# Rotary scores over 128 rows with zero-padded keys, and three planner costs raised, in a two-layer hybrid decoder

## The chip, the core and the metric

The kernel runs on one core of one Trainium2 chip. The time is the device time of one execution in microseconds; of several runs the median counts. One execution was taken with the hardware profiler, and the rows below are from that one.

## The reference, cut

Two layers over 512 tokens of width 1024. Each layer is a half-step SwiGLU feed-forward (hidden width 2816), a mixer of three branches (gated DeltaNet, Conformer convolution, latent attention), and a second half-step feed-forward, with a layer norm behind each. The change is in the latent attention: its scores are the sum of a 128-wide product of each head and a 64-wide rotary product, whose key is shared by all four heads.

```python
def causal_block_attention(q_nope, q_rope, k_nope, k_rope, v):
    t = q_nope.shape[1]
    scale = (MLA_NOPE + MLA_ROPE) ** -0.5
    outs = []
    for i in range(t // ATTN_BLOCK):
        q0, q1 = i * ATTN_BLOCK, (i + 1) * ATTN_BLOCK
        s = (jnp.einsum('bqhd,bkhd->bhqk', q_nope[:, q0:q1], k_nope[:, :q1])
             + jnp.einsum('bqhr,bkr->bhqk', q_rope[:, q0:q1], k_rope[:, :q1])).astype(jnp.float32) * scale
        mask = jnp.arange(q1)[None, :] <= jnp.arange(q0, q1)[:, None]
        p = jax.nn.softmax(jnp.where(mask, s, -jnp.inf), axis=-1).astype(v.dtype)
        outs.append(jnp.einsum('bhqk,bkhv->bqhv', p, v[:, :q1]))
    return jnp.concatenate(outs, axis=1)
```

The DeltaNet branch squares and normalizes its keys and queries after a short convolution, and scales the keys by per-token factors; the planner costs that are raised are those of such scalings.

## The kernel before

Nothing is issued where it is written. Every engine instruction goes through a proxy into `Planner._record`, which notes an estimated cost in ns (`_cost`), what it reads and writes, and a priority: the running sum of TensorE costs at that place, plus a bias. `plan` then simulates the five queues with these costs, and at each point gives an engine the ready instruction of highest priority whose buffer is free. `issue` emits them all in the order of the simulated starts; this is why nearly every row of the profile has one line, L287. On the chip each engine runs its own list strictly in that order. So a changed cost or one changed instruction can move any instruction of the neighbourhood, and an instruction whose operands come later than planned holds up what stands behind it on its engine.

Most multiplications are three float32r products of a number split into a high and a low part (`mm3`, one TensorE instruction each). The scores, the products of the delta rule and P times V are in plain float32, for which TensorE runs two instructions per product. The tiles called `s` are slots of 128x512 float32 in SBUF, of which 76 rotate; `ps` are the eight PSUM banks; `xh` and `xl` are the two parts of the layer's input; `raw` are weights as loaded.

Each mixer begins with the key heads: projection, `short_conv` (a ScalarE scaling and three VectorE steps over 511, 510 and 509 columns, then a tanh and a product of 512 columns), transposes, and the squares. From the sums of squares VectorE makes the factors `rky`; ScalarE scales `ktok` by them in quarters (`scale_quarters`, 16 instructions a layer there), TensorE transposes the scaled quarters and makes `kk`; VectorE forms `U` and, in blocks of 32 partitions, `comp3`. Then the query heads go the same way: short convolution, and a group of four transposes per head.

In the attention part, head `h` and row block `i` of 128 tokens have `n = (i + 1) * 128` keys. `ps[:, 0:n]` gets two products: `qn[h]` with `kn[h]` over 128 rows of the array, and the rotary one over 64 rows. `qr[h // 2]` holds the rotary queries of an even head in partitions 0 to 63 and of the next odd head in 64 to 127; `krope` holds the same 64 key rows twice, in both halves. Then VectorE adds the mask, takes the maximum and scales it, ScalarE makes the exponentials and their sum, VectorE the reciprocal and the scaled P, TensorE transposes P, ScalarE copies it out, and TensorE multiplies with V (8 instructions a head, over 512, 384, 256 and 128 columns). Other work of VectorE is put between: splits of weights, and the 30 shifted steps for each of the four channel groups of the Conformer convolution.

Of the kernel before, what the change touches and what calls it, by code (L numbers as in the profile page):

```python
# [35 lines left out]
class Planner:  # L36
# [64 lines left out]
    def _cost(self, engine, name, outs, ins, k):  # L101
        o = outs[0]
        n = 1
        for d in o.shape[1:]:
            n *= d
        psum = any(x.space == bass.MemoryType.PSUM for x in ins)
        if engine == "PE":
            if name == "transpose":
                return 109.0
            if k["rhs"].dtype == F32R:  # L110
                return 13.4 + n / 2.4
            part = o.shape[0] < 128 or k["lhsT"].shape[0] < 128
            return max(8.0 + n / 0.6, 116.0) + (100.0 if part else 0.0)
        vectors = 0
        if engine in ("DVE", "POOL"):
            vectors = sum(x.free_size() == 1 for x in ins[1:])
            if n == 1:
                vectors = len(ins) - {"tensor_scalar": 1, "scalar_tensor_tensor": 2}.get(name, len(ins))
        if engine == "DVE":
            if name == "reciprocal":  # L120
                return 70 + 8.3 * n
            fast = name in ("tensor_scalar", "tensor_copy") and not psum
            if name in ("bn_stats", "bn_aggr", "reduce_max"):
                n = max(n, ins[0].free_size())
            return 70 + 57 * min(vectors, 1) + n * (0.52 if fast else 1.04)
        if engine == "ACT":
            c = (52 if psum else 94) + 0.83 * max(n, 64)
            if o.shape[0] < 128 and o.shape[0] % 32 == 0:
                c += 110
            c += 93 * sum(hasattr(k.get(x), "tensor") for x in ("scale", "bias", "accum_out"))  # L130
            return c
        if engine == "POOL":
            return 125 + n * {"tensor_tensor": 2.15, "tensor_scalar": 0.9}.get(name, 1.0)
        return max(500.0, n * o.shape[0] * 4 / 200.0)
# [209 lines left out]
def trunk(tc, a, out):  # L344
    pl = Planner(tc)

    with ExitStack() as ctx:
# [9 lines left out]
        def slot(dtype=F32, share=None):  # L357
            return pl.tile(s_p, [128, 512], dtype, "s", N_SLOTS, share)
# [16 lines left out]
        V, S, G, PE, Q = pl.V, pl.S, pl.G, pl.PE, pl.Q  # L375
# [380 lines left out]
        def mixer(l):  # L756
# [85 lines left out]
            for h in (2, 3):  # L842
                w = wcols(C_DK + h * 128)
                ps = bank()
# [14 lines left out]
            for h in range(H):  # L859
# [17 lines left out]
                for j in range(4):  # L877
                    u = 4 * h + j
                    c = slice(j * 128, (j + 1) * 128)
# [6 lines left out]
            for h in range(H):  # L886
                w = wcols(C_DQ + h * 128)
                ps = bank()
# [6 lines left out]
                for j in range(4):  # L895
                    c = slice(j * 128, (j + 1) * 128)
# [27 lines left out]
            for h in range(H):  # L924
                glu_taps(h)
                w = wcols(C_DV + h * 128)
                ps = bank()
# [45 lines left out]
            for h in range(H):  # L973
                y, x, n = spread(y3, h), spread(x3, h), slot()
# [9 lines left out]
            for tt in range(NT):  # L984
                o = slot()
                rs, vns, news = slot(), slot(), slot()
                c = slice(tt * 128, (tt + 1) * 128)
                for h in range(H):
                    u = 4 * h + tt
                    hc = slice(h * 128, (h + 1) * 128)  # L990
                    ps = bank()
                    q = quarters(ps)
                    rhs = vtok[h][:, c]
                    if tt:
# [3 lines left out]
                        rhs = r  # L998
# [50 lines left out]
            scale = small([128, 4], "scale", 1)  # L1049
# [3 lines left out]
            ps = bank()  # L1053
# [26 lines left out]
                S.copy(kr[64 * g:64 * g + 64], kr_sb[0:64])  # L1080
            krope = rope(kr, swapped(kr_sb, (0, 0)))


            og = []
            for h in range(H):
                w = wcols(C_DZ + h * 128)
                ps = bank()
# [7 lines left out]
            for h in range(H):  # L1095
                ps = bank()
# [6 lines left out]
            qn, qr, kn, vv = [], [], [], []  # L1103
# [45 lines left out]

            ao = []  # L1150
            for h in range(H):
                hr = slice(64 * (h % 2), 64 * (h % 2) + 64)
                pt = [slot() for _ in range(4)]
                for i in range(NT):
                    n = (i + 1) * 128
                    c = slice(i * 128, n)
                    ps = bank()
                    PE.matmul(ps[:, 0:n], lhsT=qn[h][:, c], rhs=kn[h][:, 0:n], start=True, stop=False)
                    PE.matmul(ps[:, 0:n], lhsT=qr[h // 2][hr, c], rhs=krope[hr, 0:n], start=False, stop=True)
                    V.tensor_tensor(ps[:, c], ps[:, c], C("amask"), op=ADD)  # L1160
                    mx = small([128, 1], "mx")
                    V.reduce_max(mx, ps[:, 0:n], axis=mybir.AxisListType.X)
                    V.tensor_scalar(mx, mx, scale[:, i:i + 1], -1.0, op0=MUL, op1=MUL)
                    p = slot()
                    rs = small([128, 1], "rs")
                    S.activation(p[:, 0:n], ps[:, 0:n], AF.Exp, scale=scale[:, i:i + 1], bias=mx, accum_out=rs)
                    V.reciprocal(rs, rs)
                    V.tensor_scalar(p[:, 0:n], p[:, 0:n], rs, None, op0=MUL)
                    tp = bank()
                    transposes(tp, quarters(p)[:i + 1])  # L1170
                    for j in range(i + 1):
                        S.copy(pt[j][:, c], quarters(tp)[j])
                ps = bank()
                for j in range(NT):
                    PE.matmul(ps[:, j * 128:], lhsT=vv[j][:, h * 128:(h + 1) * 128], rhs=pt[j][:, j * 128:],
                              start=j == 0, stop=j == NT - 1)
                ao.append(split(ps))
# [119 lines left out]
```

## Time and profile before

| what | value |
|---|---|
| median of 3 runs | 2466.42 us (2465.38 to 3408.69) |
| the profiled execution | 2464.4 us, span 2462.6 us |
| TensorE clock granted, mean | 0.998 |
| TensorE / VectorE / ScalarE / POOL busy | 99% / 83% / 51% / 0% |
| HBM | 108 GB/s over the span |

The span is the time from the first to the last instruction; the execution's own time lies 1.8 us above it. The third run, 3408.69 us, stands alone, and the median does not depend on it. In the profile PE is TensorE's multiplications and PEld its weight loads, DVE is VectorE, ACT ScalarE.

### The profile page before, as it was taken

The page shows a single profiled execution, that of the slowest core. Times are in us where ns is not written, and L with a number is a line of the kernel's source. Part 1 is how long each engine was busy: PE and PEld are TensorE (multiplying, and loading weights), DVE is VectorE, ACT ScalarE, POOL GpSimd, SP SyncE. Part 2 cuts the span into 40 slices and gives each one's busy share as a digit, 9 for nine tenths or more (in the row PEclk, how much of TensorE's full clock was granted, in tenths as well). Part 3 has the DMA queues.
Part 4 walks back from the last instruction along what each step waited for, and adds up shares of the span by engine and source line. Part 5 has one row for each costly group of instructions (what it writes and reads, how often), then busy time and mean ns, then how long its engine had stood idle before and what let it go on. Part 6 is the DMA issues. An engine that isn't in the chain of part 4 may idle for free.

```text
span 2462.6 us, 41114 instructions
## 1 busy us (share of the span) xinstructions
PE 2438.4 (99%) x15860; PEld 2207.6 (90%) x15860; DVE 2044.8 (83%) x4197; ACT 1267.1 (51%) x2781; POOL 0.2 (0%) x4
## 2 busy tenths in 40 slices
PE   8999999999999999999999999999999999999998
PEld 8999887888799899998899998878878998999986
DVE  7998467999999799984699883689999987999844
ACT  6655328436646446553356552383366464565530
POOL 0000000000000000000000000000000000000000
PEclk9999999999999999999999999999999999999999
DMA  5434452312233623344333353513122335233431
GB/s 164 115 109 142 131 145 82 94 53 72 83 98 102 190 78 108 107 125 141 120 95 104 110 172 101 155 51 103 34 81 86 104 103 180 86 104 105 146 121 49
DMA packets 268804, 267.71 MB, mean 109 GB/s; under 512 B 17652, under 2 KB 220608, under 8 KB 268608
## 3 DMA queue, kind: packets, MB, share of 16 engines
q1 hardware_dynamic: 268608, 265.08, 36.0%
q8 instruction: 124, 2.03, 0.3%
q14 instruction: 72, 0.59, 0.1%
HBM read 247.74 MB, written 17.30 MB: 108 GB/s over the span
## 4 chain that ended last, share of the span: by engine, by line
PE 95%; DVE 2%; ACT 2%; issue 0%; DMA 0%; SPq 0%; DVEq 0%; ACTq 0%
PE ps L287 95%; DVE s L287 2%; ACT s L287 1%; ACT ps L287 0%; ACT xh L287 0%; DMA s<-in_x 0%; DVE xl L287 0%; DVE lnt L287 0%; DVE lny L287 0%; SPq L287 0%; DVE st L287 0%; DVEq L1293 0%; DVE mv L287 0%; DVE lnv L287 0%; DVE neg_eg L287 0%
## 5 line engine op out<-in xcount | busy, mean ns | idle before, releaser
L287 PE MATMUL ps<-s 128*128 128x256 f32 (+3 forms) x9212 | 1561.3, 324 | 0.0
L287 PEld LDWEIGHTS ps<-s 128*128 128x128 f32 (+1 forms) x9212 | 1351.2, 190 | 154.8 <-issue 17.0
L287 PE MATMUL ps<-xh,s 128*128 128x256 f32 (+2 forms) x4064 | 900.2, 308 | 2.8 <-ACT s L287 1.8
L287 PEld LDWEIGHTS ps<-xh,s 128*128 128x128 f32 (+1 forms) x4064 | 678.2, 191 | 36.5 <-ACT s L287 2.2
L287 DVE TENSOR_TENSOR s<-raw,s 128x512 fp32r<-128x512 f32 (+1 forms) x844 | 548.8, 681 | 138.0 <-PE ps L287 53.3
L287 PE MATMUL ps<-xl,s 128*128 128x256 f32 (+2 forms) x2032 | 623.6, 307 | 0.1
L287 DVE TENSOR_TENSOR s<-s 128x512 fp32r<-128x512 f32 (+10 forms) x1014 | 591.3, 612 | 29.1 <-ACT s L287 13.7
L287 ACT CAST s<-raw 128x512 fp32r<-128x512 f32 (+1 forms) x740 | 433.9, 619 | 225.4 <-PE ps L287 162.1
L287 ACT CAST s<-s 128x512 fp32r<-128x512 f32 (+1 forms) x642 | 358.4, 593 | 221.4 <-DVE s L287 189.9
L287 ACT COPY s<-ps 128x256 f32<-128x256 f32 (+3 forms) x664 | 257.4, 400 | 379.8 <-PE ps L287 378.0
L287 PEld LDWEIGHTS ps<-xl,s 128*128 128x128 f32 (+1 forms) x2032 | 387.2, 191 | 17.6 <-DVE xl L287 0.5
L287 DVE SCALAR_TENSOR_TENSOR s<-s 128x512 f32<-128x512 f32 (+26 forms) x356 | 249.7, 712 | 1.4 <-ACT s L287 1.1
L287 DVE TENSOR_TENSOR s<-ps,s 128x256 f32<-128x256 f32 (+1 forms) x336 | 147.5, 439 | 87.9 <-PE ps L287 74.7
L287 ACT ACTIVATE s<-s 128x512 f32<-128x512 f32 x162 | 103.3, 667 | 84.6 <-DVE s L287 83.5
L287 DVE SCALAR_TENSOR_TENSOR s<-s,ps 128x512 f32<-128x512 f32 x96 | 64.6, 680 | 91.5 <-PE ps L287 89.9
L287 DVE TENSOR_TENSOR s<-raw 128x512 f32<-128x512 f32 x208 | 139.6, 683 | 0.0
L287 PE MATMUL ps<-ident,s 128*128 128x128 f32 (+1 forms) x508 | 86.5, 284 | 12.1 <-DVE s L287 4.7
L287 PEld LDWEIGHTS ps<-ident,s 128*128 128x128 f32 (+1 forms) x508 | 61.3, 143 | 36.2 <-issue 12.7
L287 ACT CAST xh<-ps 128x512 fp32r<-128x512 f32 x48 | 28.6, 595 | 126.5 <-PE ps L287 126.4
L287 DVE TENSOR_TENSOR s<-s,raw 128x512 f32<-128x512 f32 x104 | 71.0, 683 | 0.1
L287 DVE SCALAR_TENSOR_TENSOR s<-ps,s 128x510 f32<-128x510 f32 (+3 forms) x88 | 63.1, 739 | 2.1 <-PE ps L287 1.7
L287 ACT ACTIVATE s<-ps,s 128x512 f32<-128x512 f32 x58 | 40.3, 718 | 45.0 <-PE ps L287 44.6
(100 smaller groups left out, 552.0 us busy)
## 6 DMA issues: line engine op xcount, KB each, us to landing
raw<-in_w_in SPq DMA_DIRECT2D x106, 512.0 KB, 3.9
raw<-in_ffn_w_gate SPq DMA_DIRECT2D x88, 512.0 KB, 3.7
raw<-in_ffn_w_up SPq DMA_DIRECT2D x88, 512.0 KB, 3.8
raw<-in_ffn_w_down SPq DMA_DIRECT2D x88, 512.0 KB, 4.9
spill<-s SPq DMA_DIRECT2D x40, 256.0 KB, 2.0
s<-spill SPq DMA_DIRECT2D x40, 256.0 KB, 2.6
raw<-in_w_out SPq DMA_DIRECT2D x16, 512.0 KB, 4.3
s<-in_x SPq DMA_DIRECT2D x16, 256.0 KB, 3.8
```

Of the source, the lines that this page charges most:

```text
L287: self.issued = o["f"](*o["a"], **o["k"])
```

## The change

The rotary keys are kept in two tiles: `krope` with its lower half cleared, for the even heads, and `kr2` with its upper half cleared, for the odd ones. Each rotary product then goes over all 128 rows, with the rotary queries of both heads of the pair as one operand; the other head's queries meet zeros. New are one VectorE copy of 64x512 and two clears of 64x512 on POOL in each layer; the clear of `krope` comes behind the copy. In the planner, a rotary product no longer has the 100 ns for a part of the array; a VectorE instruction on fewer than 128 partitions counts 90 ns more; and ScalarE instructions count 93 ns for each further tile that they read, so that the scalings `S.mul` by a column, which had none so far, now do, and 126 in place of 93 for a sum that they write.

```diff
@@ -122,12 +122,13 @@
             fast = name in ("tensor_scalar", "tensor_copy") and not psum
             if name in ("bn_stats", "bn_aggr", "reduce_max"):
                 n = max(n, ins[0].free_size())
-            return 70 + 57 * min(vectors, 1) + n * (0.52 if fast else 1.04)
+            part = 90 if o.shape[0] < 128 else 0
+            return 70 + part + 57 * min(vectors, 1) + n * (0.52 if fast else 1.04)
         if engine == "ACT":
             c = (52 if psum else 94) + 0.83 * max(n, 64)
             if o.shape[0] < 128 and o.shape[0] % 32 == 0:
                 c += 110
-            c += 93 * sum(hasattr(k.get(x), "tensor") for x in ("scale", "bias", "accum_out"))
+            c += 93 * (len(ins) - 1) + 126 * (len(outs) - 1)
             return c
@@ -1080,6 +1081,12 @@
                 S.copy(kr[64 * g:64 * g + 64], kr_sb[0:64])
             krope = rope(kr, swapped(kr_sb, (0, 0)))
 
+            kr2 = slot()
+            G.memset(kr2[0:64], 0.0)
+            V.tensor_copy(kr2[64:128], krope[64:128])
+            G.memset(krope[64:128], 0.0)
+            kropes = krope, kr2
+
@@ -1149,14 +1156,13 @@
             for h in range(H):
-                hr = slice(64 * (h % 2), 64 * (h % 2) + 64)
                 pt = [slot() for _ in range(4)]
                 for i in range(NT):
                     n = (i + 1) * 128
                     c = slice(i * 128, n)
                     ps = bank()
                     PE.matmul(ps[:, 0:n], lhsT=qn[h][:, c], rhs=kn[h][:, 0:n], start=True, stop=False)
-                    PE.matmul(ps[:, 0:n], lhsT=qr[h // 2][hr, c], rhs=krope[hr, 0:n], start=False, stop=True)
+                    PE.matmul(ps[:, 0:n], lhsT=qr[h // 2][:, c], rhs=kropes[h % 2][:, 0:n], start=False, stop=True)
```

The order of the instructions moves in the two mixers; the feed-forward parts keep theirs on TensorE. Three places follow; lines are L287 before and L288 now.

TensorE at the first scores of layer 0. Before, the four blocks of head 0 (`s_1408`, `s_1406` are its query and key, `s_1330` the rotary queries of heads 0 and 1, `s_1376` the rotary key), the last two of them shown, and then transposes of P between the blocks of head 1 (`s_1415`, `s_1413`):

```order
L287 MATMUL ps_1444<-s_1408,s_1406 128x384
L287 MATMUL ps_1444<-s_1330,s_1376 128x384
L287 MATMUL ps_1449<-s_1408,s_1406 128x512
L287 MATMUL ps_1449<-s_1330,s_1376 128x512
L287 MATMUL ps_1438<-ident_75,s_1436 128x128
L287 MATMUL ps_1461<-s_1415,s_1413 128x128
L287 MATMUL ps_1461<-s_1330,s_1376 128x128
```

The same place now (`s_1332` is the second key tile, `s_1377` the rotary queries):

```order
L288 MATMUL ps_1445<-s_1409,s_1407 128x384
L288 MATMUL ps_1445<-s_1330,s_1377 128x384
L288 MATMUL ps_1450<-s_1409,s_1407 128x512
L288 MATMUL ps_1450<-s_1330,s_1377 128x512
L288 MATMUL ps_1462<-s_1416,s_1414 128x128
L288 MATMUL ps_1462<-s_1332,s_1377 128x128
L288 MATMUL ps_1467<-s_1416,s_1414 128x256
L288 MATMUL ps_1467<-s_1332,s_1377 128x256
L288 MATMUL ps_1472<-s_1416,s_1414 128x384
L288 MATMUL ps_1439<-ident_75,s_1437 128x128
```

Two and a half further blocks of head 1 now stand ahead of the first transpose of P.

VectorE at the end of the short convolution of query head 0, layer 0, before (`s_1021` and `s_1022` are head 0's convolution and its tanh, `s_1031` and `s_1041` the convolutions of heads 1 and 2, `raw_1079` a weight):

```order
L287 TENSOR_TENSOR s_994<-s_1014,s_912 32x128
L287 SCALAR_TENSOR_TENSOR s_1031<-ps_1030,s_915,s_1031 128x510
L287 SCALAR_TENSOR_TENSOR s_1022<-s_1022,s_1021 128x512
L287 SCALAR_TENSOR_TENSOR s_1031<-ps_1030,s_915,s_1031 128x509
L287 SCALAR_TENSOR_TENSOR s_1041<-ps_1040,s_915,s_1041 128x511
L287 TENSOR_TENSOR s_1081<-raw_1079,s_1080 128x512
L287 SCALAR_TENSOR_TENSOR s_1041<-ps_1040,s_915,s_1041 128x510
L287 TENSOR_TENSOR s_996<-ps_1024,s_996 128x512
L287 TENSOR_TENSOR s_1022<-s_1022,s_997 128x512
L287 SCALAR_TENSOR_TENSOR s_1032<-s_1032,s_1031 128x512
```

The same place now:

```order
L288 TENSOR_TENSOR s_994<-s_1014,s_912 32x128
L288 SCALAR_TENSOR_TENSOR s_1022<-s_1022,s_1021 128x512
L288 SCALAR_TENSOR_TENSOR s_1031<-ps_1030,s_915,s_1031 128x510
L288 SCALAR_TENSOR_TENSOR s_1041<-ps_1040,s_915,s_1041 128x511
L288 SCALAR_TENSOR_TENSOR s_1031<-ps_1030,s_915,s_1031 128x509
L288 TENSOR_TENSOR s_996<-ps_1024,s_996 128x512
L288 TENSOR_TENSOR s_1022<-s_1022,s_997 128x512
L288 SCALAR_TENSOR_TENSOR s_1032<-s_1032,s_1031 128x512
```

The product that ends head 0 (`s_1022`) now stands one convolution step earlier, and a weight split and another step have left the stretch up to head 1's (`s_1032`).

TensorE at the transposes of query head 0, layer 0, before (`ps_1023`; `ps_1050` is the projection of query head 3):

```order
L287 MATMUL ps_1023<-ident_75,s_1022 128x128 x4
L287 MATMUL ps_1024<-s_1022,s_987 128x128 x4
L287 MATMUL ps_1050<-xh_76,s_1048 128x512
L287 MATMUL ps_1050<-xl_77,s_1048 128x512
L287 MATMUL ps_1050<-xh_76,s_1049 128x512
```

And now:

```order
L288 MATMUL ps_1050<-xh_76,s_1048 128x512
L288 MATMUL ps_1050<-xl_77,s_1048 128x512
L288 MATMUL ps_1050<-xh_76,s_1049 128x512
L288 MATMUL ps_1023<-ident_75,s_1022 128x128 x4
L288 MATMUL ps_1024<-s_1022,s_987 128x128 x4
```

The rest of head 3's projection has gone ahead of the transposes. Counted from the mixer's start, six float32r products of 512 columns more stand ahead of them, one of the six already ahead of the first transpose of the scaled keys.

## Rows read from the trace of the kernel before

**Rows 1.** The page: busy time of each engine, and the chain that ended last.

```profile
PE 2438.4 (99%) x15860; PEld 2207.6 (90%) x15860; DVE 2044.8 (83%) x4197; ACT 1267.1 (51%) x2781; POOL 0.2 (0%) x4
...
PE 95%; DVE 2%; ACT 2%; issue 0%; DMA 0%; SPq 0%; DVEq 0%; ACTq 0%
```

**Rows 2.** Stretches of layer 0's mixer; columns PE, PEld, DVE, ACT, POOL busy, clock, DMA.

```profile
380.00:430.00 50.00, 46.12 (x248) 37.52 (x247) 40.12 (x115) 43.10 (x133) 0.00 (x0) 1.00 0.17 45
...
600.00:660.00 60.00, 60.00 (x271) 39.67 (x271) 55.15 (x149) 42.08 (x130) 0.00 (x0) 1.00 0.22 62
...
760.00:860.00 100.00, 100.00 (x640) 91.27 (x639) 77.95 (x134) 55.72 (x107) 0.00 (x0) 1.00 0.50 153
```

**Rows 3.** Weight loads of the whole span by shape (rows*columns of the array).

```profile
L287 PEld LDWEIGHTS ps<-s 128*128 128x128 f32 x9148 | 1341.8, 190 | 142.5 <-ACT s L287 6.0 <-issue 5.6 <-DVE s L287 0.2
...
L287 PEld LDWEIGHTS ps<-s 64*128 64x128 f32 x64 | 9.4, 184 | 12.3 <-issue 11.3
```

**Rows 4.** Weight loads in time in the scores, layer 0 (start, length, what).

```profile
614.01 0.29 PEld L287 LDWEIGHTS ps<-s 64*128 64x128 f32 x2 [0.33 <-issue]
614.64 0.30 PEld L287 LDWEIGHTS ps<-s 128*128 128x128 f32 x2 [0.33 <-issue]
615.48 0.29 PEld L287 LDWEIGHTS ps<-s 64*128 64x128 f32 x2 [0.55 <-issue]
616.32 0.30 PEld L287 LDWEIGHTS ps<-s 128*128 128x128 f32 x2 [0.54 <-ACT s L287]
617.38 0.29 PEld L287 LDWEIGHTS ps<-s 64*128 64x128 f32 x2 [0.76 <-issue]
618.43 0.14 PEld L287 LDWEIGHTS ps<-ident,s 128*128 128x128 f32 x1 [0.76 <-issue]
```

**Rows 5.** Multiplications in time, the P times V of one head, layer 0.

```profile
644.16 2.36 PE L287 MATMUL ps<-s 128*128 128x512 f32 x8
646.36 0.27 PE L287 MATMUL ps<-ident,s 128*128 128x128 f32 x1
```

**Rows 6.** Multiplications in time, start of the mixer, layer 0.

```profile
408.82 0.91 PE L287 MATMUL ps<-ident,s 128*128 128x128 f32 x3 [1.25 <-ACT s L287]
...
424.59 0.61 PE L287 MATMUL ps<-xh,s 128*128 128x512 f32 x2
425.04 0.39 PE L287 MATMUL ps<-xl,s 128*128 128x512 f32 x1
425.27 0.39 PE L287 MATMUL ps<-xh,s 128*128 128x512 f32 x1
427.70 0.63 PE L287 MATMUL ps<-ident,s 128*128 128x128 f32 x4 [2.04 <-DVE s L287]
```

**Rows 7.** The same, layer 1.

```profile
1629.93 0.91 PE L287 MATMUL ps<-ident,s 128*128 128x128 f32 x3 [1.25 <-ACT s L287]
...
1649.76 0.63 PE L287 MATMUL ps<-ident,s 128*128 128x128 f32 x4 [2.07 <-DVE s L287]
```

**Rows 8.** VectorE in time, ahead of 427.70.

```profile
426.20 0.75 DVE L287 SCALAR_TENSOR_TENSOR s<-ps,s 128x510 f32<-128x510 f32 x1
426.87 0.68 DVE L287 SCALAR_TENSOR_TENSOR s<-s 128x512 f32<-128x512 f32 x1
```

**Rows 9.** VectorE in time, fourth block of the first head's softmax, layer 0.

```profile
622.59 0.30 DVE L287 TENSOR_TENSOR ps<-ps,s 128x128 f32<-128x128 f32 x1 [0.64 <-PE ps L287]
...
623.19 0.48 DVE L287 TENSOR_SCALAR s<-s,rs 128x512 f32<-128x512 f32 x1
```

**Rows 10.** Multiplications in time, last transposes of that head.

```profile
624.88 0.77 PE L287 MATMUL ps<-ident,s 128*128 128x128 f32 x5
```

**Rows 11.** Work on whole and half tiles by shape, whole span.

```profile
L287 DVE TENSOR_SCALAR s<-s 128x512 f32<-128x512 f32 x30 | 12.8, 425 | 3.9 <-ACT s L287 3.6
...
L287 ACT COPY s<-s 64x512 f32<-64x512 f32 x4 | 2.4, 612 | 0.0
```

## The prediction

> **What bounds the kernel now.** I read the page first: TensorE is busy in 99% of the span and makes 95% of the chain that ended last; VectorE has 83%, ScalarE 51% [rows 1]. So an edit is worth what it takes off TensorE's list, or off the few places where TensorE waits. Next the stretches of a mixer. From 600 to 660 and from 760 to 860 us TensorE has no gap at all; the gaps are at the mixer's start, 50 - 46.12 = 3.9 us between 380 and 430 [rows 2]. In time they are mainly two: 1.25 us in front of the first transposes of the scaled keys, released by ScalarE, and 2.04 us in front of the transposes of query head 0, released by VectorE [rows 6]. Layer 1 has the same two, 1.25 and 2.07 us [rows 7]. VectorE is second: 55.15 of 60 us in the attention stretch, but only 77.95 of 100 us between 760 and 860 [rows 2].
>
> A busy TensorE can still lose time inside its instructions. Weight loads show this: 9148 full loads have 142.5 us of idle time in front of them, 16 ns each, while the 64 loads over 64 rows have 12.3 us, 192 ns each, put down to "issue", so to no other engine [rows 3].
>
> **Term 1: no more changes between 64 and 128 rows.** First what such a product costs when nothing changes. P times V of one head is eight instructions over 512, 384, 256 and 128 columns, two each: 20 units of 128 columns from 644.16 to 646.36, 2.20 us, 0.110 us a unit [rows 5]. Now the scores, where 64 and 128 rows alternate. From 614.01 to 618.43 there are five pairs of 256, 384, 384, 512 and 512 columns, 32 units, which would take 3.52 us; they take 4.42 [rows 4]. The 0.90 us over are 0.18 us for each of five changes. Pair by pair it is 0.17 to 0.19 whatever the columns: 0.63 for 4 units, 1.05 for 8. In each pair the two loads go off close together and the next pair's loads wait until the multiplication in front is through (idle 0.33, 0.55, 0.76 us, growing with the columns).
>
> There are 4 heads x 4 blocks x 2 layers = 32 rotary products, each with a change in and a change out: 64 x 0.18 = 11.5 us on TensorE. The change leaves the columns as they are and makes every product a 128-row one, which is what P times V is; the changes go altogether. Bounds: 64 x 0.17 = 10.9, and the 12.3 us of idle time. I take **-11.5**, since it comes from the time that the pairs really take.
>
> **Term 2: the mixer's start.** The planner now counts the 16 scalings and the 32-partition blocks longer, and puts other work under them. In the new order five more float32r products stand between the first transposes of the scaled keys and those of query head 0. Three such take 425.27 - 424.59 = 0.68 us [rows 6], so 1.1 us of cover come in under the 2.04 us wait. On VectorE one step less, 0.67 us (426.20 to 426.87), stands ahead of the product that this wait is for [rows 8]. Against it, VectorE's work there begins with `kk`, which stands, by my count, some 0.35 us later in TensorE's list. So the wait could fall by 1.1 + 0.67 - 0.35 = 1.4 us, and the 1.25 us wait by the 0.2 us of one product. But VectorE works without a pause there, and what follows for TensorE is the product of query head 1, which TensorE now reaches sooner: half a microsecond or so of the gain comes back as a wait there. I take 1.0 us a layer, **-2**; the bounds are -3.4 (2 x 1.7, nothing comes back) and +2 (VectorE's chain starts later and nothing is gained, 1 us a layer).
>
> **Term 3: the softmax without its cushion.** The planner counted 100 ns for a rotary product's part of the array; the chip took 2 x 180. So each block ran 0.26 us behind the plan on TensorE, and VectorE and ScalarE had that as slack. Now it is gone. Up to the last block of the first head, P is ready at 623.67 (623.19 + 0.48) and transposed at 624.88, a margin of 1.2 us [rows 9, 10]. Eight blocks stand ahead of that transpose before, 8 x 0.36 = 2.9 us that TensorE now arrives sooner; two more blocks (128 and 256 columns, 12 units, 1.3 us) now stand ahead. VectorE itself waited for TensorE there (0.64 us in one place [rows 9]) and will be sooner too, by up to that idle time: 4.85 us in the 60 of the stretch [rows 2]. So the margin ends near nothing, and I expect short waits, about 1 us a layer, **+2**. Bounds: 0, and VectorE's floor, which is a rival below.
>
> **The other edits cost nothing that lasts.** The copy of 64x512 on VectorE, twice, is bounded by 425 ns for a whole tile of 512 columns and by ScalarE's 612 ns for the same shape [rows 11], so 0.9 to 1.2 us in the run, under the 4.85 us of VectorE's idle time. The two clears a layer go to POOL, which has nothing else to do. The clear of `krope` waits for the copy, and TensorE's first rotary product waits for the clear: a new wait, with everything on TensorE queued behind it. No row shows a POOL clear of this size; by the nearest row, 612 ns for a 64x512 copy on ScalarE, it takes about that, between 0.4 and a few us. In the new order 16 VectorE instructions of a whole tile stand between the copy and the first mask addition, some 10 us at 0.6 each, so the cover is wide; were it gone, the price would be the clear itself, once a layer. The raised costs change no work. On SyncE one weight load passes the two loads of the rotary tables, with nothing waiting.
>
> **The sum.** -11.5 - 2 + 2 = -11.5 us on the profiled execution's 2464.4 gives 2452.9. That execution lies 2.0 us below the median of 2466.42, so the forecast is **2454.9 us**, 0.5% faster.
>
> **Rivals.** *VectorE becomes the bound in the attention.* The stretch of 60 us cannot be shorter than VectorE's 55.15 us and the copy's 0.43 [rows 2, 11], unless the convolution steps between move out to the slack behind 760. The list is fixed, and by my count the part from the first mask addition to the last scaled P holds 102 VectorE instructions in both orders, so they did not. Then a layer gains 60 - 55.6 = 4.4 us, and nothing at the start: 2464.4 - 8.8 = 2455.6, with the 2.0 us 2457.6; if in addition the start's two late waits of 2.04 and 2.07 us double, 2461.7. For it: VectorE's share. Against it: its instructions in that stretch also include tail work that can slide.
>
> *Slower: transposes of P come ahead of P.* The new order packs blocks of the next head ahead of the transposes; each head has about three groups of transposes, 24 in the run. If P comes 0.8 us after TensorE on each, 24 x 0.8 = 19.2 us replace what is won: 2464.4 - 11.5 - 2 + 19.2 = 2470.1, with the 2.0 us 2472.1. It decides from 13.5 / 24 = 0.56 us a group. For it: the margin of 1.2 us was made by the very time that is removed. Against it: TensorE had no gap there, VectorE had several, and the added blocks are cover.
>
> *The change does not do what it says: padded loads wait just as well.* If a 128-row load could not slip under a running multiplication, the 64 rotary instructions would each show their load of 0.19 us [rows 3], 12.2 us, and term 1 would be gone: about 2466. Against it stand the 9148 full loads with 16 ns in front of each. In the Trainium skill, "TensorE: Matmul & The Clock Gate", section "The mechanism", loads are said to overlap running matmuls only where the row group differs; by that rule full-row loads would wait behind one another and half-row ones of alternate heads would not, which is this rival. The trace says the opposite: the full loads hide, the half-row ones wait 192 ns.
>
> **How the numbers follow.** Forecast 2450 to 2457, chance 0.60; VectorE bound, 2457 to 2464, 0.22; padded loads or gains lost elsewhere, about 2466, 0.05; slower, 2467 to 2475, 0.08; better than 2450, with term 1 at 12.3 and term 2 at 3.4 and no term 3 (2464.4 - 15.7 = 2448.7, or 2450.7 with the offset), 0.05. The range 2448 to 2464 leaves out the slower case and the one at 2466. About 2% is what a measurement of this kernel can tell from no change, 49 us here; no case reaches it on the fast side, and on the slow side only a run such as the 3408.69 would: faster 0.01, same 0.97, slower 0.02.
>
> **What would show it.** Term 1: no 64-row loads, 64 128-row ones in their place without idle time in front, and a pair of 512 columns in 0.88 us instead of 1.05. Term 2: the waits of 1.25 and 2.04 us shorter, and perhaps a new one at query head 1. Term 3: TensorE gaps in front of transposes of P, released by VectorE, of 0.1 to 1 us, some 2 us in all; more than 5 us there make the VectorE rival right, more than 13 us the slower one. A wait of TensorE for POOL would show the cover of the clears gone. Gaps in the delta rule or behind the attention, where I expect none, would make the prediction wrong in a way that I have not priced.

## The result, and the profile after

| | before | after |
|---|---|---|
| median | 2467.15 us (4 runs, 2465.38 to 3408.69) | 2446.65 us (4 runs, 2445.79 to 2447.03) |
| ratio, 95% interval | | 0.9919 [0.9899, 0.9938] |
| profiled execution, span | 2464.4, 2462.6 us | 2447.03, 2445.3 us |
| granted clock, mean | 0.998 | 0.999 |

The kernel is faster by 0.8%: less than 2%, as forecast, but the time lies 8.2 us below the forecast of 2454.9 and 1.35 us below the low end of its range, 2448. The interval ends 0.6% short of no change, so the prediction's 2% as what a measurement of this kernel can tell was too coarse. The single run at 3408.69 us is not in the ratio, and without it the median of before is 2466.42.

The page of after, busy times and the shares of the chain that ended last, beside [rows 1]:

```profile
PE 2423.1 (99%) x15860; PEld 2209.8 (90%) x15860; DVE 2043.2 (84%) x4199; ACT 1262.9 (52%) x2781; POOL 2.3 (0%) x8
...
PE 94%; DVE 3%; ACT 2%; DMA 0%; issue 0%; SPq 0%; DVEq 0%; ACTq 0%
```

TensorE has the same 15860 instructions and is busy 15.3 us less (2438.4 to 2423.1): most of the gain lies inside its busy time, where a list of waits does not show it. So I cut layer 0's mixer at five starts that both kernels have: **A** from the mixer's start to the first transpose of the scaled keys, **B** to the transposes of query head 0, **C** to the first one-column product, **D** (the delta rule) to the first score, **E** to the end of the last head's P times V. The windows of before (length, then busy us and records of PE, PEld, DVE, ACT, POOL, then clock, DMA share, GB/s):

```profile
360.94:408.82 47.88, 45.79 (x297) 40.48 (x295) 36.99 (x101) 29.69 (x87) 0.00 (x0) 1.00 0.45 129
408.82:427.70 18.88, 16.84 (x92) 13.41 (x92) 13.72 (x39) 18.80 (x52) 0.00 (x0) 1.00 0.04 11
427.70:520.98 93.28, 93.28 (x442) 77.35 (x443) 93.15 (x225) 44.34 (x99) 0.00 (x0) 1.00 0.30 78
520.98:612.66 91.68, 91.68 (x568) 80.82 (x568) 89.90 (x213) 49.61 (x132) 0.00 (x0) 1.00 0.21 63
612.66:653.43 40.77, 40.77 (x168) 23.43 (x167) 37.53 (x112) 26.04 (x93) 0.00 (x0) 1.00 0.27 78
```

The same five of after:

```profile
362.52:410.09 47.57, 45.91 (x297) 40.73 (x295) 37.08 (x101) 29.39 (x86) 0.52 (x1) 1.00 0.46 133
410.09:427.41 17.32, 16.69 (x96) 14.28 (x97) 12.96 (x38) 16.95 (x49) 0.00 (x0) 1.00 0.02 5
427.41:519.20 91.79, 91.79 (x437) 76.38 (x438) 91.72 (x218) 46.40 (x103) 0.00 (x0) 1.00 0.30 79
519.20:611.14 91.94, 91.59 (x567) 81.07 (x567) 91.31 (x220) 46.13 (x126) 0.52 (x1) 1.00 0.23 68
611.14:648.01 36.87, 36.87 (x178) 26.30 (x177) 36.70 (x115) 30.40 (x104) 0.00 (x0) 1.00 0.25 73
```

The order has moved instructions across these cuts, so lengths alone mislead. In after A holds one float32r instruction of 512 columns more, B five more, C six fewer, E nine of 512 and one of 256 columns more. What counts is the **time over the columns**: a stretch's length less 0.107 us for each 256 columns of a float32r instruction and each 128 columns of any other (0.1067 before rounding; the step between 256 and 512 columns, 0.120 and 0.227 us, and the 0.110 of [rows 5], are this rate). For E it is 36.87 - 40.77 - (9 x 0.213 + 0.107) = -5.93. In us, by kernel (the experiments follow, with layer 0 of each; their layer 1 is within 0.07 of it, but where the clock fell in one layer alone, last section: padding alone has 7.27 in C of layer 1, and the third experiment 4.58 in B of layer 1):

| kernel | A | B | C | D | E |
|---|---|---|---|---|---|
| before, layer 0 | 6.64 | 4.59 | 5.82 | 8.04 | 6.85 |
| before, layer 1 | 6.68 | 5.54 | 5.81 | 8.03 | 6.85 |
| after, layer 0 | 6.13 | 1.96 | 5.60 | 8.31 | 0.92 |
| after, layer 1 | 6.13 | 1.96 | 5.59 | 8.28 | 0.91 |
| padding alone | 6.64 | 4.59 | 5.84 | 8.05 | 2.05 |
| costs alone | 6.14 | 1.95 | 5.58 | 7.45 | 6.81 |
| rotary first in every second block | 6.68 | 5.53 | 5.78 | 8.08 | 4.91 |
| ScalarE costs alone | 6.13 | 3.25 | 7.24 | 7.02 | 6.91 |
| VectorE cost alone | 6.63 | 3.46 | 6.02 | 7.76 | 6.85 |
| change, old count of the rotary product | 6.15 | 1.95 | 5.64 | 8.29 | 1.99 |

After less before, layers 0 and 1 together: A -1.06, B -6.21, C -0.44, D +0.52, E -11.87, in all -19.1 us. The span fell by 17.3, since the profiled execution of after began worse: its first mixer starts at 362.52 instead of 360.94, and all of these 1.6 us arise in the first 17 us of the program, which the change does not touch (0.9 behind the first loads of `in_x`, 0.7 because TensorE's first products go at half pace up to 16.6 us, before up to 13.9). Other executions need not start so; by the medians the fall is 20.5, or 19.8 from 2466.42, which is near the 19.1.

**E, the scores.** The weight loads of after in layer 0's first blocks, which answer to [rows 4]:

```profile
614.17 0.19 PEld L288 LDWEIGHTS ps<-s 128*128 128x128 f32 x1 [0.24 <-issue]
614.60 0.19 PEld L288 LDWEIGHTS ps<-s 128*128 128x128 f32 x1 [0.24 <-issue]
615.03 0.19 PEld L288 LDWEIGHTS ps<-s 128*128 128x128 f32 x1 [0.24 <-issue]
615.46 1.50 PEld L288 LDWEIGHTS ps<-s 128*128 128x128 f32 x9 [0.24 <-issue]
```

In a block of 512 columns a load goes off every 0.43 us, one multiplication ahead. The pair of instructions takes 0.86 us, where [rows 4] had 1.05. And over the whole span, for [rows 3] and [rows 11]:

```profile
L288 PEld LDWEIGHTS ps<-s 128*128 128x128 f32 x9212 | 1349.7, 190 | 144.6 <-issue 5.4 <-ACT s L288 3.7 <-DVE s L288 1.8
...
L288 POOL MEMSET s<- 64x512 f32 x4 | 2.1, 522 | 1813.3 <-PE ps L288 1366.2 <-DVE s L288 447.1
L288 DVE COPY s<-s 64x512 f32<-64x512 f32 x2 | 0.9, 426 | 0.1
```

9212 full loads with 16 ns of idle time each: the 64 new ones added 2.1 us to the sum of idle time where the old ones had 12.3.

**A and B, the mixer's start.** TensorE, layer 0 and then layer 1, for [rows 6] and [rows 7]:

```profile
410.09 0.33 PE L288 MATMUL ps<-ident,s 128*128 128x128 f32 x1 [0.84 <-ACT s L288]
...
411.09 0.27 PE L288 MATMUL ps<-ident,s 128*128 128x128 f32 x1
411.11 0.49 PE L288 MATMUL ps<-xh,s 128*128 128x512 f32 x1
411.44 0.27 PE L288 MATMUL ps<-ident,s 128*128 128x128 f32 x1
411.47 0.48 PE L288 MATMUL ps<-xh,s 128*128 128x512 f32 x1
...
427.41 0.63 PE L288 MATMUL ps<-ident,s 128*128 128x128 f32 x4 [0.63 <-DVE s L288]
...
1622.12 0.33 PE L288 MATMUL ps<-ident,s 128*128 128x128 f32 x1 [0.87 <-ACT s L288]
1639.43 0.63 PE L288 MATMUL ps<-ident,s 128*128 128x128 f32 x4 [0.67 <-DVE s L288]
```

The wait of 1.25 us is 0.84, that of 2.04 is 0.63. That is 1.82 us of the 3.14 that A and B gained. Of the rest 1.22 lies in B, between the transposes of the scaled keys, and 0.10 in A. Each follows a ScalarE scaling; before they stood in rows of two and three, here a float32r product often stands between them. TensorE before, some 4 us behind the first row of [rows 6]:

```profile
412.80 0.53 PE L287 MATMUL ps<-ident,s 128*128 128x128 f32 x2
413.16 0.39 PE L287 MATMUL ps<-s 128*128 128x128 f32 x2
413.39 0.81 PE L287 MATMUL ps<-ident,s 128*128 128x128 f32 x3
414.04 0.83 PE L287 MATMUL ps<-s 128*128 128x128 f32 x6
```

And ScalarE before, in the same place:

```profile
411.94 1.88 ACT L287 ACTIVATE s<-s,rky 128x128 f32<-128x128 f32 x6
413.70 0.59 ACT L287 COPY s<-ps 128x512 f32<-128x512 f32 x1
```

Six scalings take 413.70 - 411.94 = 1.76 us, 0.29 each. Three transposes from 413.39 take 0.65 us, where three times their columns are 0.32. TensorE is shown busy all the while: the pause between two transposes is too short to be listed as idle. In after a transpose and a product of 512 columns alternate there, a transpose every 0.35 us (411.09, 411.44), 0.32 of it columns: longer than the 0.29 of a scaling, so TensorE does not wait for ScalarE.

### The profile page after: what moved, and what is told of

It is laid out like the page before. It is cut to its first block, busy times and chain, and to the rows that moved or that the text cites. A ratio compares the mean times of both kernels' runs of the same rounds, so it can differ in the third digit from the quotient of the medians.

```text
span 2445.3 us, 41139 instructions
## 1 busy us (share of the span) xinstructions
PE 2423.1 (99%) x15860; PEld 2209.8 (90%) x15860; DVE 2043.2 (84%) x4199; ACT 1262.9 (52%) x2781; POOL 2.3 (0%) x8
## 4 chain that ended last, share of the span: by engine, by line
PE 94%; DVE 3%; ACT 2%; DMA 0%; issue 0%; SPq 0%; DVEq 0%; ACTq 0%
PE ps L288 94%; DVE s L288 3%; ACT s L288 1%; ACT ps L288 0%; DMA raw<-in_ffn_w_gate 0%; ACT xh L288 0%; DVE xl L288 0%; DVE lnt L288 0%; DVE lny L288 0%; SPq L288 0%; DVE st L288 0%; DVEq L1299 0%; DVE mv L288 0%; DVE lnv L288 0%; DVE neg_eg L288 0%
## 5 line engine op out<-in xcount | busy, mean ns | idle before, releaser
L288 PE MATMUL ps<-s 128*128 128x256 f32 (+3 forms) x9212 | 1548.7, 324 | 0.7 <-DVE s L288 0.5
L288 PEld LDWEIGHTS ps<-s 128*128 128x128 f32 x9212 | 1349.7, 190 | 144.6 <-issue 5.4
L288 PE MATMUL ps<-xh,s 128*128 128x256 f32 (+2 forms) x4064 | 900.2, 308 | 3.4 <-ACT s L288 2.4
L288 PEld LDWEIGHTS ps<-xh,s 128*128 128x128 f32 (+1 forms) x4064 | 678.9, 191 | 38.5 <-ACT s L288 2.8
L288 DVE TENSOR_TENSOR s<-raw,s 128x512 fp32r<-128x512 f32 (+1 forms) x844 | 547.1, 680 | 137.6 <-PE ps L288 54.4
L288 PE MATMUL ps<-xl,s 128*128 128x256 f32 (+2 forms) x2032 | 623.7, 307 | 0.1
L288 DVE TENSOR_TENSOR s<-s 128x512 fp32r<-128x512 f32 (+9 forms) x1014 | 589.9, 612 | 27.2 <-PE ps L288 13.0
L288 ACT CAST s<-raw 128x512 fp32r<-128x512 f32 (+1 forms) x740 | 434.1, 620 | 224.9 <-PE ps L288 160.0
L288 ACT CAST s<-s 128x512 fp32r<-128x512 f32 (+1 forms) x642 | 358.2, 594 | 213.4 <-DVE s L288 177.2
L288 ACT COPY s<-ps 128x256 f32<-128x256 f32 (+3 forms) x664 | 256.7, 401 | 379.4 <-PE ps L288 374.2
L288 PEld LDWEIGHTS ps<-xl,s 128*128 128x128 f32 (+1 forms) x2032 | 387.4, 191 | 18.4 <-DVE xl L288 0.5
L288 DVE SCALAR_TENSOR_TENSOR s<-s 128x512 f32<-128x512 f32 (+25 forms) x356 | 249.2, 711 | 1.4 <-ACT s L288 1.1
L288 DVE TENSOR_TENSOR s<-ps,s 128x256 f32<-128x256 f32 (+1 forms) x336 | 147.2, 438 | 84.4 <-PE ps L288 76.0
L288 DVE SCALAR_TENSOR_TENSOR s<-s,ps 128x512 f32<-128x512 f32 x96 | 64.4, 680 | 90.8 <-PE ps L288 89.7
L288 ACT ACTIVATE s<-s 128x512 f32<-128x512 f32 x162 | 102.2, 665 | 73.2 <-DVE s L288 72.5
L288 DVE TENSOR_TENSOR s<-raw 128x512 f32<-128x512 f32 x208 | 139.2, 682 | 0.0
L288 ACT CAST xh<-ps 128x512 fp32r<-128x512 f32 x48 | 28.6, 595 | 127.8 <-PE ps L288 127.8
L288 PE MATMUL ps<-ident,s 128*128 128x128 f32 (+1 forms) x508 | 84.6, 278 | 8.8 <-DMA s<-in_x 4.8
L288 PEld LDWEIGHTS ps<-ident,s 128*128 128x128 f32 (+1 forms) x508 | 61.5, 143 | 23.9 <-issue 8.3
L288 DVE TENSOR_TENSOR s<-s,raw 128x512 f32<-128x512 f32 x104 | 70.9, 681 | 0.1
L288 ACT ACTIVATE s<-ps,s 128x512 f32<-128x512 f32 x58 | 40.0, 721 | 50.1 <-PE ps L288 50.1
L288 DVE SCALAR_TENSOR_TENSOR s<-ps,s 128x510 f32<-128x510 f32 (+3 forms) x88 | 62.7, 739 | 0.3
```

Of the source, the lines that this page charges most:

```text
L288: self.issued = o["f"](*o["a"], **o["k"])
```

## The experiments

All were run beside the kernel before on the same chip; ratios are to it, with the 95% interval. The planner's lines are those of the diff ahead.

**Padding alone.** All costs old; the rotary product still counts the 100 ns for a part of the array:

```diff
-            part = o.shape[0] < 128 or k["lhsT"].shape[0] < 128
+            part = o.shape[0] < 128 or k["lhsT"].shape[0] < 128 or k["rhs"].tensor.name in self.padded
...
+            pl.padded |= {krope.tensor.name, kr2.tensor.name}
```

> Rotary products padded to 128 rows as in the change, all planner costs as before (a rotary product still counted 100 ns longer, so that the order moves little). Theory A: the padding gives the 64 changes of the array times 0.18 to 0.19 us, about -12 us, and nothing at the start of the mixers: 2454 to 2456 against 2466.5, with the waits in front of the transposes of query head 0 still near 2 us. Theory B: the padding gives the whole gain of 20 us, since a faster attention also shortens what follows: 2446 to 2449.

Measured: 2456.96 us against 2466.2, 0.9964 [0.9952, 0.9977]. E falls by 4.80 us a layer, the other stretches of layer 0 keep their times to 0.02. (In layer 1 of this execution the clock fell in C, where before had it fall in B; last section.) TensorE's two waits stay:

```profile
409.15 0.91 PE L288 MATMUL ps<-ident,s 128*128 128x128 f32 x3 [1.23 <-ACT s L288]
...
428.03 0.63 PE L288 MATMUL ps<-ident,s 128*128 128x128 f32 x4 [2.06 <-DVE s L288]
```

So the padding acts in the scores and nowhere else; it does not act through the order of the mixer's start. That is theory A in its place, but not in its size: E gives 9.6 us for the two layers where 12 were expected, and the time lies 1 us above its range. The 1.1 us a layer by which E at 2.05 lies above the 0.92 of after are taken up in the sixth experiment.

**The raised costs alone.** 64-row products as before, both cost lines as in the change.

> Rotary products over 64 rows as before, with both raised costs (ScalarE's and VectorE's). Theory A: about -7.5 us, 2458 to 2460, all of it between the start of a mixer and its query heads; 64-row loads keep 12 us of idle time. Theory B: no gain, 2465 to 2468.

Measured: 2456.16 us against 2466.2, 0.996 [0.9947, 0.9972]. The two waits are those of after:

```profile
409.06 0.33 PE L288 MATMUL ps<-ident,s 128*128 128x128 f32 x1 [0.85 <-ACT s L288]
...
426.37 0.63 PE L288 MATMUL ps<-ident,s 128*128 128x128 f32 x4 [0.64 <-DVE s L288]
```

About half of the gain is thus the planner's: theory A's place again, and 2 us more than its range, of which D, where it expected nothing, gives 0.59 a layer. The product of the two ratios, 0.9964 x 0.996 = 0.9924, is the change's 0.9919 within the intervals: the halves add up in the total. Stretch by stretch they do not: the change has 1.1 us a layer less in E, and 0.85 more in D, than the two make together.

**Fewer changes of rows, no padding.** Blocks 1 and 3 issue the rotary product first, so that two 64-row products meet; per layer 22 changes instead of 32, the rest of the order as before:

```diff
-                    PE.matmul(ps[:, 0:n], lhsT=qn[h][:, c], rhs=kn[h][:, 0:n], start=True, stop=False)
-                    PE.matmul(ps[:, 0:n], lhsT=qr[h // 2][hr, c], rhs=krope[hr, 0:n], start=False, stop=True)
+                    both = [(qn[h][:, c], kn[h][:, 0:n]), (qr[h // 2][hr, c], krope[hr, 0:n])][::1 - 2 * (i % 2)]
+                    for j, (q, r) in enumerate(both):
+                        PE.matmul(ps[:, 0:n], lhsT=q, rhs=r, start=not j, stop=bool(j))
```

> As before, but in blocks 1 and 3 of each head the rotary product comes first and the other second, so that products over 64 rows stand side by side where the planner allows it: 44 changes between 64 and 128 rows in place of 64, in an otherwise equal order. Theory A, the cost sits in the change: 20 x 0.18 = -3.6 us, 2462 to 2464. Rival: the cost sits in every product over 64 rows, whose loads can't go ahead: no difference, 2466 to 2467.5.

Measured: 2461.88 us against 2466.2, 0.9981 [0.9972, 0.999]. The 64-row loads are as many as before, with their idle time nearly halved from the 12.3 us of [rows 3]:

```profile
L287 PEld LDWEIGHTS ps<-s 64*128 64x128 f32 x64 | 9.3, 185 | 6.7 <-issue 3.9 <-PE ps L287 0.3 <-ACT s L287 0.3
```

E falls by 6.85 - 4.91 = 1.94 us for ten changes, 0.19 each, with the number of 64-row products unchanged, and the 22 left make 4.91 - 0.92 = 3.99, 0.18 each. It is the change between 64 and 128 rows that costs, not the 64-row product: theory A, with the time 0.1 us below its range.

**ScalarE costs alone.** The kernel before with the one line of the ScalarE cost.

> As before, with ScalarE's raised costs alone. Theory A1: the scalings of the keys, 0.29 us apart on ScalarE, were planned too short, and putting other products between the transposes that wait for them gives most of the gain at the mixers' start: -4 to -6 us, 2460 to 2462, with the transposes of the scaled keys no longer in rows of two or three. Theory A2: the gain there is VectorE's 32-partition blocks planned longer: -1 us at most, 2465 to 2467.

Measured: 2458.66 us against 2466.2, 0.9971 [0.9959, 0.9982].

```profile
408.78 0.33 PE L287 MATMUL ps<-ident,s 128*128 128x128 f32 x1 [0.85 <-ACT s L287]
...
426.11 0.63 PE L287 MATMUL ps<-ident,s 128*128 128x128 f32 x4 [2.00 <-DVE s L287]
```

The first wait falls to 0.85 and B by 1.34 us although its wait stays at 2.00: these are the pauses between the transposes, as theory A1 has it, with a fall of 7.5 us where it had 4 to 6. The delta rule (D) gains 1.0 us, which the full change does not keep. The profiled execution, 2460.78 us, is the slowest of the seven; in it the clock fell in C of both layers (last section).

**VectorE cost alone.** The kernel before with the 90 ns for fewer than 128 partitions.

> Rotary products over 64 rows, VectorE's raised cost for work on fewer than 128 partitions alone. Theory: this cost moves the transposes of query head 0 behind what VectorE really does ahead of them, and the wait of 2.0 us there falls to about 0.8, while the short pauses between the transposes of the scaled keys and the wait of 1.25 us ahead of them stay: -3 to -5 us, 2461 to 2463, the more so as a clock drop behind the long wait goes with it. Rival: the query wait is ScalarE's and goes with ScalarE's costs only: 2465 to 2467.

Measured: 2462.35 us against 2465.07, 0.9987 [0.9979, 0.9996].

```profile
409.12 0.91 PE L288 MATMUL ps<-ident,s 128*128 128x128 f32 x3 [1.23 <-ACT s L288]
...
427.51 0.63 PE L288 MATMUL ps<-ident,s 128*128 128x128 f32 x4 [0.87 <-DVE s L288]
```

The complement: the first wait stays, the second falls to 0.87, the pauses stay, as the theory has it; the fall of 2.7 us is a little less than its 3 to 5.

**The change with the old count of the rotary product.** Padded as in the change, costs raised, but the product still counts 100 ns more, as in the first experiment.

> The whole change, but the planner still counts a padded rotary product 100 ns longer. Theory: the list is then made for a TensorE that is slower than the chip's, P comes late at its transposes as in the run with the padding alone, and the attention of each layer takes 1.1 us more than in the change: 2448 to 2450 against 2446.5. Rival: those waits came from the old ScalarE and VectorE costs: 2446 to 2447.

Measured: 2448.48 us against 2465.07, 0.9933 [0.9919, 0.9946]. E takes 1.07 us a layer more than in after, as the theory has it; one gap is listed in layer 0, the rest is too short for it:

```profile
637.17 0.73 PE L289 MATMUL ps<-ident,s 128*128 128x128 f32 x5 [0.24 <-DVE s L289]
```

The intervals overlap with that of the change, so the total alone does not tell them apart; E does, in both layers. Padding alone, which counts the same way, has the 1.1 us as well. There P is seen to be late: a row of five transposes of P takes 0.91 us, where the row of five ahead of it (622.69) takes 0.71, and within it VectorE ends the scaled P of 384 columns only at 626.22 (625.81 + 0.41). Before, the last transposes of head 0 had a margin of 1.2 us [rows 9, 10]. VectorE and TensorE, padding alone:

```profile
625.81 0.41 DVE L288 TENSOR_SCALAR s<-s,rs 128x384 f32<-128x384 f32 x1
...
625.91 0.91 PE L288 MATMUL ps<-ident,s 128*128 128x128 f32 x5
```

**The sums of squares counted at their length.** On ScalarE a square with its sum (`ssk`) takes 0.40 us from start to start, which the changed planner counts shorter. The wait at the end of A is for scalings that stand behind these sums. The change with

```diff
-            c += 93 * (len(ins) - 1) + 126 * (len(outs) - 1)
+            c += 93 * (len(ins) - 1) + (242 if len(outs) > 1 and outs[1].tensor.name.startswith("ssk") else 126) * (len(outs) - 1)
```

> The whole change, and the squares of the key heads with their sums planned at the 0.40 us that one takes on ScalarE, 116 ns more than the change plans. Theory: the wait of about 0.9 us ahead of the transposes of the scaled keys is these eight squares' shortfall and goes; -1 to -2 us, 2444.5 to 2445.5. Rival: no difference or a worse order elsewhere, 2446 to 2449.

Measured: 2456.16 us against 2465.07, 0.9962 [0.995, 0.9975]: slower than the change by 9.5 us by the medians, outside the theory's range and the rival's: a miss. That wait is gone (A 4.87 instead of 6.13), but the delta rule takes 14.37 over its columns instead of 8.31, with waits of TensorE that after does not have:

```profile
554.21 19.49 PE L288 MATMUL ps<-s 128*128 128x128 f32 x163 [1.27 <-DVE s L288]
...
575.99 1.42 PE L288 MATMUL ps<-s 128*128 128x128 f32 x8 [0.50 <-ACT s L288]
...
582.69 0.75 PE L288 MATMUL ps<-s 128*128 128x128 f32 x4 [0.66 <-DVE s L288]
```

These three make 2.4 of the 6.1 us; the rest was not traced. A better number for one instruction gave a worse list somewhere else.

**The same with 150 and with 200** in place of 242.

> The whole change, with a sum of squares of the key heads counted 150 ns in place of 126, so that the order in the delta rule stays closer to that of the change than it did with 242. Theory: each order has its own waits in the delta rule, and only the wait ahead of the scaled keys follows from this cost: it falls by 8 x 0.024 = 0.2 us a layer, 2446 to 2447, and what the total does beyond that shows in the stretch from the latent sums to the scores. Rival: any larger cost here ruins the delta rule, 2452 or more.

> The same with 200 ns. Theory: the wait ahead of the scaled keys falls by about 0.6 us a layer, 2445 to 2446 where the delta rule stays as in the change. Rival: 2452 or more, the loss in the delta rule again.

Measured against 2466.32: 2445.41 us with 150, 0.9916 [0.9903, 0.993]; 2449.14 with 200, 0.9931 [0.9919, 0.9944]. With 150 the wait at the end of A is 0.57 and D keeps 8.32; with 200 the wait is gone and D takes 11.17. So the wait at the end of A follows this cost, as expected (0.27 us less where 0.2 was). The total with 200 lies between the theory's range and the rival's, since D loses part of what it lost with 242. The 2445.41 is the lowest median of all, but its interval overlaps that of the change, so it is not shown to be faster.

```profile
408.94 0.33 PE L288 MATMUL ps<-ident,s 128*128 128x128 f32 x1 [0.57 <-ACT s L288]
```

## Why the prediction was wrong, point by point

**The failed step is term 2, "the mixer's start", taken as -2 with bounds of -3.4 and +2.** What it expected came, shorter waits under a list that puts other work between; its size did not, and the working for the larger wait was wrong in its parts. A, B and C gave -7.7 us in the run (-3.36 and -4.35 a layer). Where it comes from, as far as the runs show:
- The waits fell by 0.41 + 1.41 us in layer 0 and 0.38 + 1.40 in layer 1, 3.6 us. The working had 0.2 for the first one and 1.4 for the second. That the 1.4 came out to a hundredth is luck, as the rows below the list show.
- The step that turned 1.6 a layer into 1.0 was "half a microsecond or so of the gain comes back as a wait" at query head 1. It does not: C behind it is shorter by 0.22 us in each layer.
- The pauses between transposes were left out, because a row with no idle time in front of it was read as a full one: 1.2 us a layer in B. The run with the ScalarE costs alone shows them by themselves, 1.34 us in B with its wait at 2.00.
- In layer 1 before, TensorE ran at half clock behind the first wait, which put B at 5.54 instead of 4.59, 0.95 us (last section). The row of layer 1 [rows 7] was read only for its wait.

These make 3.6 + 2.4 + 0.44 + 0.95 = 7.4 of the 7.7. Even the bound of -3.4 could not hold: it took the two listed waits for all there was.

The parts of the 1.4: VectorE's first work on `kk` and its end of query head 0, and TensorE's last product ahead of the transposes of that head. VectorE before, then VectorE and TensorE of after:

```profile
413.00 1.13 DVE L287 SCALAR_TENSOR_TENSOR s<-ps,beta,s 128x128 f32<-128x128 f32 x4 [4.83 <-PE ps L287]
...
413.90 1.13 DVE L288 SCALAR_TENSOR_TENSOR s<-ps,beta,s 128x128 f32<-128x128 f32 x4 [4.24 <-PE ps L288]
...
426.58 0.69 DVE L288 SCALAR_TENSOR_TENSOR s<-s 128x512 f32<-128x512 f32 x1
...
426.39 0.39 PE L288 MATMUL ps<-xh,s 128*128 128x512 f32 x1
```

Take all from the first transpose of the scaled keys, 408.82 before and 410.09 in after. The five products of 1.1 us came in as cover, but the pauses that went are 1.2 us, so TensorE ends its work ahead of the wait after 16.69 us (426.39 + 0.39) where [rows 6] has 16.84 (425.27 + 0.39): 0.15 sooner, not 1.1 later. VectorE begins on `kk` after 3.81 us instead of 4.18, 0.37 sooner where the working had 0.35 later, and from there to the end of head 0 (426.58 + 0.69, before 426.87 + 0.68 [rows 8]) takes 13.37 us instead of 14.55, where the working had 0.67 less. It is thus done 1.55 us sooner; the wait fell by 1.55 - 0.15 = 1.40, and the working had reached the same number by 1.1 + 0.67 - 0.35.

**Term 3, "the softmax without its cushion", +2, did not come.** TensorE has no listed wait in E of after, and E's 0.92 us over the columns leave no room for it: at the prediction's own 0.18 a change, 6.85 - 32 x 0.18 = 1.09 would be left of before's. The working took the margin of 1.2 us at [rows 10] and let the eight earlier blocks eat it. Yet time of that size is lost, 1.1 us a layer, in the two kernels whose planner still counts 100 ns for a product that no longer takes them; only 0.24 of it is a listed wait (sixth experiment). With the count removed the planner placed the blocks of the next head further ahead, and nine float32r instructions more ahead of the last P times V. So that the cushion is gone does not by itself cost the time; the count does. That the blocks and instructions placed ahead are what covers them is read from the order and was not tried by itself.

**Term 1, -11.5, was right.** E gives -11.87 for 64 changes, 0.185 each, against the 0.18 read from pairs; the ten changes of the third experiment give 0.19. The Trainium skill, "TensorEngine Tiling (Array Packing)", section "Key Properties", says that changing the tiling mode drains TensorE; the traces fit that, since the 64-row loads stand idle for 192 ns each until the multiplication in front is through [rows 3, 4], and they put the price at 0.18 to 0.19 us a change here.

**What had no term:** D, the delta rule, +0.5 us, where I expected no gaps. The costs alone shorten D by 0.6 a layer, padding alone leaves it; only both together lengthen it. One gap of 0.27 us is listed in after; which moved instruction makes the rest was not traced.

**The other edits at nothing** held: the copy takes 0.9 us in the run, as bounded, a clear on POOL 0.52, and no TensorE wait is put down to POOL.

The sum thus: -11.9 for terms 1 and 3 together where -9.5 stood, -7.7 for -2, +0.5 for 0, in all -19.1 for -11.5.

**The rivals.** *VectorE becomes the bound*: no, but nearly: it is busy 36.70 of the 36.87 us of E in after, against 37.53 of 40.77 before, and TensorE has no gap. From this I infer, without a run, that the next microsecond off TensorE in E would have to come off VectorE as well, or part of VectorE's work would have to move. *Transposes of P ahead of P*: no such waits. *Padded loads wait just as well*: refuted by the 9212 loads, 16 ns of idle time each. The prediction gave the rule behind it only in part: the Trainium skill, "TensorE: Matmul & The Clock Gate", section "The mechanism", also lets a load go ahead of running multiplications into the background weight buffer, which the full-row loads fit; its other sentence, overlap only where the row group differs, does not describe them. *Better than 2450*, the case nearest to what came, had a chance of 0.05: it left term 3 out, as the run did, but stopped at 3.4 for term 2.

## What to carry to other kernels

When a list's order changes, sum the gaps inside "busy" too: cut both traces at the same starts and take each stretch's length less its columns, since pauses of 0.2 us between instructions paced by another engine are on no list of waits. A short product over 64 rows between 128-row ones costs two changes of some 0.18 us each, and zeros in the spare rows cost TensorE nothing here. A planner's count that is wrong in one place should be tried as a dial with the whole time as its measure: the true length of the squares was the worst of the values tried. And a wait that comes out as reckoned does not show that the parts of the reckoning were right: cut it into when the one engine arrives and when the other is done.

## What the runs showed of the hardware that was not expected

Behind some waits at the mixer's start the granted clock falls to 0.50, the 1.2 GHz level, for 3.4 us, though TensorE is busy all that time. Before, layer 1, behind the wait of 1.25 us (windows, columns as above):

```profile
1618.00:1632.00 14.00, 12.64 (x59) 9.27 (x59) 8.98 (x31) 13.68 (x51) 0.00 (x0) 1.00 0.44 113
1632.00:1635.40 3.40, 3.40 (x15) 3.21 (x15) 0.00 (x0) 2.92 (x9) 0.00 (x0) 0.50 0.02 5
1635.40:1640.00 4.60, 4.60 (x37) 4.43 (x36) 4.36 (x15) 4.26 (x12) 0.00 (x0) 1.00 0.00 0
```

With the ScalarE costs alone, layer 0, behind the wait of 2.00 us:

```profile
424.00:427.30 3.30, 1.30 (x12) 1.22 (x12) 3.21 (x7) 3.27 (x9) 0.00 (x0) 1.00 0.01 2
427.35:430.70 3.35, 3.35 (x11) 2.68 (x10) 3.35 (x6) 2.33 (x9) 0.00 (x0) 0.50 0.00 0
430.80:434.00 3.20, 3.20 (x21) 2.82 (x21) 1.80 (x4) 2.84 (x10) 0.00 (x0) 1.00 0.00 0
```

11 multiplications are recorded in 3.35 us at 0.50, 21 in the 3.20 us behind, though not all of one size. It costs 0.95 us in the first case (B of layer 1 against B of layer 0) and about 1.4 in the second (C at 7.24, against the 5.82 of before). It came also in layer 1 of that run, in padding alone (layer 1) and in the third experiment (layer 0), each time 0.1 to 2.1 us behind the end of such a wait, and not behind every one: before, layer 0 has the same two waits and no fall, and the VectorE cost alone keeps that of 1.23 and 1.24 us in its two layers without one. In after no mixer shows it, nor with the costs alone; there the longest wait left is 0.87 us. So a wait of one or two microseconds can cost some 0.7 of its length again behind it, and part of what a removed wait returns is this.
